# The end of a hybrid attention, state-space and expert block: gate matmuls, weight splits and the final scaling in another order

## The chip, the cores and the metric

The kernel runs on one core of a Trainium2 chip. The metric is the device time of one execution in microseconds. TensorE (PE) does the matmuls, VectorE (DVE), ScalarE (ACT) and GpSimd (POOL) the rest, and SyncE (SP) issues the loads and stores. TensorE's clock has two levels, 2.4 and 1.2 GHz; the profile shows the granted one as 1.00 or 0.50.

## The reference

One token block of 256 x 1024 goes through a norm, an attention branch and a state-space branch, a mixture of 16 experts, and at the end a gated projection of a second input and a last norm. What the change touches is the end:

```python
        h2 = rms_norm(x, ffn_norm_g[i])
        x = x + hier_moe(h2, w_rg[i], b_rg[i], w_re[i], b_re[i], w_gate[i], w_up[i], w_down[i])
        x = x + jax.nn.sigmoid(x @ w_ple_gate[i]) * (p[i] @ w_ple_proj[i])
    return rms_norm(x, final_norm_g)
```

`hier_moe` sums, over experts, a weight per token times `(silu(h @ w_gate[e]) * (h @ w_up[e])) @ w_down[e]`. `x @ w_ple_gate` is 256 x 1024 by 1024 x 1024.

## The kernel before

The 256 tokens are two tiles `i` = 0, 1 of 128 partitions (`xt[0]`, `xt[1]`), and the 1024 columns are worked on in halves (512) or quarters (256). Experts are handled in batches; the last two batches (numbers 4 and 5, members 8 to 11 and 12 to 15) are what is left when the end begins. Their down projections bring rows of tokens that were gathered for an expert, and a matmul with a selection matrix `st` scatters them back onto the tokens:

- `half_down` (L1450) is batch 4's down projection for one half, in PE line L1455; `q_down` (L1463) is batch 5's for one quarter, PE line L1467. Both end in `q_ev` (L1445): ACT writes the scaled result's high part `yh` (L1447), DVE the remainder `yl` (L1448), so that two fast matmuls together keep full precision.
- `scatter` (PE line L1215) and `q_x2` (PE line L1531) add `yh` and `yl` onto the tokens in PSUM. `q_x2` then adds the sum to the tokens on DVE (L1535).
- `q_T` transposes the finished quarter of x on PE (L1541) and splits it into `x2h` (ACT, L1543) and `x2l` (DVE, L1544).

The gate projection has eight blocks c = 0 to 7 of 128 rows of `w_ple_gate`. Block c needs quarter c // 2 of x: blocks 4 and 5 quarter 2, blocks 6 and 7 quarter 3. `pg_split(c)` splits the block's weights into a high part `wh_pg` (ACT, L377) and a low part `wl_pg` (DVE, L380). `pg(c, i, hfs)` issues its matmuls for token tile i and the halves named: three each (L389 with `wh` and `x2h`, L390 with `wl` and `x2h`, L391 with `wh` and `x2l`). So a block is twelve matmuls of 512 columns, and all eight blocks 96. There are four PSUM accumulators, one for each tile and half; the last two blocks are therefore done accumulator by accumulator (`last_two`, L1635), so that the sigmoids can begin when the first is full.

`pg_gate` (L1567) takes the sigmoid on ACT (L1570), and multiplies and adds on DVE (L1571, L1572). `pg_sq` (L1574) sums squares on ACT (L1577), `pg_sum` (L1580) adds them on DVE (L1581), `pg_pow` (L1584) takes the power -1/2 on POOL (L1586). `pg_gain` (L1588) multiplies with the last norm's gain (L1590), `pg_out` (L1592) with gain and reciprocal root at once (L1594), `store` (L1598) issues the store on SP (L1600).

What sets the order: `manual_schedule` leaves every engine the order in which the code is written, and each engine works through its own instructions in that order, waiting on semaphores for the others. Loads are issued on SP from a list, when a slot of on-chip memory is free, eight in flight at most: four d_r (8 loads, for `half_down(..., "r", 1)`), d_2 (4 loads, for `q_down(2)`), pg 4 and 5, the gain `fng`, d_3 (4 loads, for `q_down(3)`), pg 6 and 7, in this order.

The order of the end before the change, at L1603 to L1667: all of blocks 0 to 2 and half of 3, the r half's projection, the other half of block 3, the scatter, then quarter 2 (projection, scatter, transposes), blocks 4 and 5 with quarter 3's projection among them, quarter 3's scatter and transposes, and the last two blocks.

Of the kernel before, what the change touches and what calls it, by code (L numbers as in the profile page):

```python
# [11 lines left out]
AF = mybir.ActivationFunctionType  # L12
# [17 lines left out]
NB = len(WIDTH)  # L30
# [62 lines left out]
def emit(ctx, tc, ring, x, p, mix_norm_g, w_in, conv_w, conv_b, dt_bias,  # L93
# [1114 lines left out]
    def scatter(pr, mo, st, tiles, halves=(0, 1)):  # L1208
        for i in tiles:
            for hf in halves:  # L1210
                for n, y in enumerate(("yh", "yl")):
                    j, first = 2 * i + hf, pr == 0 and n == 0
                    if first:
                        bx[j] = bank(j, f"x2_{j}")
                    pe.matmul(bx[j], st[:, i * P:(i + 1) * P], mo[y][:, 512 * hf:512 * hf + 512],  # L1215
                              start=first, stop=False, skip_group_check=True)
# [233 lines left out]
    def half_down(pr, hT, cw, n, hf):  # L1450

        b = bank(4, f"y{n}{pr}")
        for c in range(4):
            for s, e in enumerate(members(pr)):
                pe.matmul(b[part(pr, s), :], hT[:, c, part(pr, s)], ready[f"d{e}_{n}{c // 2}"][0][:, c % 2, :],  # L1455
                          start=(c == 0), stop=(c == 3), skip_group_check=True)
            if c % 2:
                for e in members(pr):
                    consumed(f"d{e}_{n}{c // 2}")
        for q in range(2):  # L1460
            q_ev(b, cw, 2 * hf + q, 256 * q)
# [86 lines left out]
    def pg_split(c):  # L1548
        pgw[c] = split(f"pg_{c}", 1) + ([],)
        lows.pop()()  # L1550

    def pg(c, i, hfs=(0, 1)):
        _, _, a, b, done = pgw[c]
        for hf in hfs:
            if c == 0:
                pgb[i, hf] = bank(2 * i, f"pg{i}") if hf == 0 else accbank(f"pg{i}1")
            w, s = slice(512 * hf, 512 * hf + 512), slice(i * P, (i + 1) * P)
            three(pgb[i, hf], X2H.k(c)[:, s], X2L.k(c)[:, s], a[:, 0, w], b[:, 0, w], c == 0, c == KD - 1, True)
            done.append(hf)
        if len(done) == 4:  # L1560
            for t in pgw[c][:2]:
                t.free()
# [26 lines left out]
        t = sc.t[i][:, 512 * h:512 * h + 512]  # L1589
        dve.tensor_tensor(t, t, ready["fng"][0][:, 0, 512 * h:512 * h + 512], OP.mult)  # L1590

    def pg_out(h):  # L1592
        t = sc.t[0][:, 512 * h:512 * h + 512]
        dve.scalar_tensor_tensor(t, t, stat[:, 40:41], ready["fng"][0][:, 0, 512 * h:512 * h + 512], op0=OP.mult,  # L1594
                                 op1=OP.mult)
        store(0, h)

    def store(i, h):  # L1598
        s = slice(512 * h, 512 * h + 512)
        sp.dma_start(dram(out, i * P * D + 512 * h, [[D, P], [1, 512]]), sc.t[i][:, s])  # L1600
# [9 lines left out]
    pg_split(2)  # L1610
    pg(0, 1)
    pg_split(3)
    for c in (1, 2):
        for i in range(2):
            pg(c, i)
    pg(3, 0)
    half_down(NB - 2, hT_a, pend[2], "r", 1)
    pg(3, 1)
    scatter(pend[0], mo, pend[1], (0, 1), (1,))
    q_down(2)  # L1620
    pg_split(4)
    q_x2(2)
    q_T(2)
    pg_split(5)
    pg(4, 0)
    pg(5, 0)
    pg(4, 1)
    q_down(3)
    pg(5, 1)
    q_x2(3)  # L1630
    pg_split(6)
    q_T(3)
    pg_split(7)

    def last_two(i, hf):  # L1635
        for c in (6, 7):
# [4 lines left out]
    last_two(0, 1)  # L1641
    pg_gate(0, 1)
    pg_sq(0, 0)
    last_two(1, 0)
    pg_gate(1, 0)
    pg_sq(0, 1)
# [5 lines left out]
    pg_sq(1, 0)  # L1652
    pg_sq(1, 1, 0)
    pg_sq(1, 1, 1)
    pg_out(0)
    pg_gain(1, 0)
    pg_sum(1)
    r = stat[:, 41:42]
    dve.tensor_tensor(r, stat[:, 38:39], r, OP.add)
    pg_pow(1)  # L1660
    pg_gain(1, 1)
    t = [sc.t[1][:, 512 * h:512 * h + 512] for h in range(2)]
    act.activation(t[0], t[0], AF.Copy, scale=r)
    dve.tensor_scalar(t[1], t[1], r, None, op0=OP.mult)
    for h in range(2):
        store(1, h)
    pg_out(1)  # L1667
    consumed("fng")
    for a in X:
        a.free()  # L1670
# [28 lines left out]
```

## Time and profile before

| | us |
|---|---|
| median of 3 runs | 505.53 (501.83 to 506.48) |
| profiled execution, its time | 504.57 |
| its span, first to last instruction | 502.5 |
| PE busy in the span | 466.6 |
| DVE, ACT, POOL busy | 210.8, 183.0, 122.8 |

Times in the rows are microseconds from the start of the span. In a timeline a row is: start, duration, engine, line, operation, output and inputs by the program's names, shapes, count, and in brackets how long the engine had been idle and what it waited for. PEld is a weight load, which runs beside the matmuls; a "q" behind an engine's name is its sequencer. Matmuls overlap, so a matmul's own duration is longer than the step from one to the next.

### The profile page before, as it was taken

Reading aid. Unit: us, or ns where it says so; the run is one execution under the profiler, and the core shown is the slowest. Engines: PE = TensorE matmul, PEld = TensorE weight load, DVE = VectorE, ACT = ScalarE, POOL = GpSimd, SP = SyncE. Lnnn points to the kernel's source line nnn. Section 1 sums busy time; section 2 is a strip of 40 time slices with the busy share of each in tenths; the row PEclk is TensorE's granted clock in tenths of the full one; section 3 lists DMA queues with packets and bytes.
Section 4 is the critical chain, followed back from the end, with each engine's and each line's share of the span. In section 5 each row is a group of like instructions: output and inputs, shape, how many; then the busy total and the mean of one; then the engine's idle time right before and its main releaser. Section 6 shows DMA issues by size and latency. Waiting matters only on the chain.

```text
span 502.5 us, 8090 instructions
## 1 busy us (share of the span) xinstructions
PE 466.6 (93%) x3001; PEld 321.6 (64%) x3001; DVE 210.8 (42%) x413; ACT 183.0 (36%) x333; POOL 122.8 (24%) x82
## 2 busy tenths in 40 slices
PE   6999999999999999999999999999999588889781
PEld 5997998999988999988744353534322111155551
DVE  5423687795669584744644111111100000060345
ACT  5546577634687263443531111111100000140233
POOL 3847535333788640050400000000000000000001
PEclk8899999999999999999999999999999899989787
DMA  9899997522323798677569999999999999999602
GB/s 294 235 348 349 348 349 232 180 71 59 112 87 125 244 400 275 233 243 302 210 208 331 393 410 407 409 409 409 410 404 394 405 410 408 390 392 372 222 0 84
DMA packets 73271, 145.25 MB, mean 289 GB/s; under 512 B 8245, under 2 KB 41353, under 8 KB 73225
## 3 DMA queue, kind: packets, MB, share of 16 engines
q1 hardware_dynamic: 73080, 144.15, 79.9%
q8 instruction: 25, 0.41, 0.3%
q10 hardware_dynamic: 144, 0.52, 0.3%
q14 instruction: 22, 0.17, 0.1%
HBM read 143.61 MB, written 1.05 MB: 288 GB/s over the span
## 4 chain that ended last, share of the span: by engine, by line
PE 66%; DMA 21%; DVE 7%; ACT 2%; issue 2%; POOL 0%; POOLq 0%; DVEq 0%; SPq 0%; ACTq 0%
DMA u<-in_w_up_dram 8%; DMA g<-in_w_gate_dram 6%; PE g L1168 6%; PE ac_gb L411 5%; PE ac_ob L411 5%; PE ac_ga L411 5%; PE u L1168 4%; PE y L1198 4%; DMA d_h<-in_w_down_dram 4%; PE ac_xs L411 3%; PE ac_q L411 3%; PE ac_bc L411 2%; PE ac_z L411 2%; PE ac_k L411 2%; PE g L1111 2%; DMA pg<-in_w_ple_gate_dram 2%
## 5 line engine op out<-in xcount | busy, mean ns | idle before, releaser
L1586 POOL TENSOR_TENSOR stat<-stat,nhalf 128x1 f32<-128x1 f32 x2 | 1.6, 786 | 250.8 <-DVE stat L1581 248.2
L1168 PE MATMUL u<-u,XT 128*64 128x512 f32 (+1 forms) x256 | 55.7, 598 | 3.3 <-DMA u<-in_w_up_dram 3.1
L1168 PE MATMUL g<-g,XT 128*64 128x512 f32 (+1 forms) x256 | 50.0, 620 | 6.5 <-PEq L1245 4.7
L1168 PEld LDWEIGHTS u<-u,XT 128*64 128x64 f32 (+1 forms) x256 | 14.2, 123 | 40.4 <-issue 21.6
L1168 PEld LDWEIGHTS g<-g,XT 128*64 128x64 f32 (+1 forms) x256 | 13.9, 127 | 40.0 <-issue 30.7
L1198 PE MATMUL y<-d,mid 128*64 128x512 f32 x128 | 28.3, 595 | 0.0
L1181 DVE SCALAR_TENSOR_TENSOR mid<-u,cwt,mid 128x512 f32<-128x512 f32 x6 | 4.5, 751 | 50.5 <-issue 49.3
L380 POOL TENSOR_TENSOR wl_xs<-xs,wh_xs 128x1024 fp32r<-128x1024 f32 x8 | 19.1, 2392 | 17.7 <-ACT wh_xs L377 12.6
L1144 ACT ACTIVATE sT<-st 128x256 fp32r<-128x256 f32 x6 | 2.3, 385 | 53.3 <-DVE cwt L1143 51.0
L1205 DVE SCALAR_TENSOR_TENSOR yl<-y,cwt,yh 128x512 fp32r<-128x512 f32 x8 | 6.0, 750 | 34.0 <-ACT yh L1204 33.6
L1140 DVE COPY cwt<-st 128x1 f32<-128x1 f32 x6 | 0.9, 158 | 45.7 <-PE st L1135 45.7
L1198 PEld LDWEIGHTS y<-d,mid 128*64 128x64 f32 x128 | 8.8, 137 | 16.7 <-issue 15.1
L759 POOL TENSOR_TENSOR su<-su,su 128x768 f32<-128x768 f32 x8 | 16.9, 2110 | 7.6 <-ACT su L758 7.1
L389 PE MATMUL pg<-wh_pg,x2h 128*128 128x512 f32 x32 | 15.2, 474 | 1.4 <-ACT x2h L1543 1.4
L1188 ACT ACTIVATE mid<-hT 128x512 f32<-128x512 f32 x5 | 3.0, 598 | 34.5 <-PE hT L1187 34.5
L380 POOL TENSOR_TENSOR wl_wo<-wo,wh_wo 128x1024 fp32r<-128x1024 f32 x3 | 7.8, 2615 | 31.0 <-ACT wh_wo L377 29.6
L390 PE MATMUL pg<-wl_pg,x2h 128*128 128x512 f32 x32 | 14.5, 452 | 0.8 <-DVE wl_pg L380 0.8
L391 PE MATMUL pg<-wh_pg,x2l 128*128 128x512 f32 x32 | 14.1, 442 | 0.0
L1204 ACT ACTIVATE yh<-y,cwt 128x512 fp32r<-128x512 f32 x8 | 5.5, 688 | 22.5 <-PE y L1198 22.5
L380 POOL TENSOR_TENSOR wl_z<-z,wh_z 128x1024 fp32r<-128x1024 f32 x4 | 9.6, 2401 | 16.3 <-ACT wh_z L377 7.1
L1119 ACT ACTIVATE XT<-g,gfd 128x256 f32<-128x256 f32 x12 | 5.0, 471 | 21.0 <-PE g L1111 19.8
L1111 PE MATMUL g<-S,h2h 128*128 128x256 f32 x44 | 11.5, 295 | 0.6 <-ACT XT L1119 0.6
(414 smaller groups left out, 1176.7 us busy)
## 6 DMA issues: line engine op xcount, KB each, us to landing
g<-in_w_gate_dram SPq DMA_DIRECT2D x64, 512.0 KB, 10.1
u<-in_w_up_dram SPq DMA_DIRECT2D x64, 512.0 KB, 10.1
d<-in_w_down_dram SPq DMA_DIRECT2D x40, 512.0 KB, 9.7
d_h<-in_w_down_dram SPq DMA_DIRECT2D x16, 512.0 KB, 10.4
xs<-in_w_in_dram SPq DMA_DIRECT2D x8, 512.0 KB, 9.9
z<-in_w_in_dram SPq DMA_DIRECT2D x8, 512.0 KB, 8.7
ga<-in_w_in_dram SPq DMA_DIRECT2D x8, 512.0 KB, 8.7
gb<-in_w_in_dram SPq DMA_DIRECT2D x8, 512.0 KB, 4.9
```

What stands on the lines that cost most here:

```text
L380: (pool if pool_lo else dve).tensor_tensor(l, src, h.bitcast(F32), OP.subtract)
L389: pe.matmul(o, lh, rh, start=start, stop=False, skip_group_check=skip)
L390: pe.matmul(o, lh, rl, start=False, stop=False, skip_group_check=skip)
L391: pe.matmul(o, ll, rh, start=False, stop=stop, skip_group_check=skip)
L411: pe.matmul(st["b"][:, T * f:T * f + T], w[:, k, 128 * f:128 * f + 128], x_.k(kk), start=(n + kk + f == 0), stop=(n == 2 and kk == 4 * k_u ...
L759: pool.tensor_tensor(e, e, cbm[:, t // 4:t // 4 + 1, :].to_broadcast([P, 2, 384]), OP.mult)
L1111: pe.matmul(b[:, 256 * k:256 * k + 256], MO[hs, i].t[0][:, kk * P:(kk + 1) * P], S, start=(first and n == 0 and k == 0), stop=(last and n ...
L1119: act.activation(o[:, 256 * k:256 * k + 256], b[:, 256 * k:256 * k + 256], AF.Copy, scale=g2[:, k:k + 1])
L1168: pe.matmul(b[part(pr, s), :], xg.k(kk)[:, part(pr, s, s0)], ready[f"{w}{e}_{c}"][0][:, k, :], start=(kk == 0), stop=(kk == KD - 1), skip_ ...
L1198: pe.matmul(by[hf][part(pr, s), :], mo["hT"][:, c, part(pr, s)], w[:, 0, 512 * hf:512 * hf + 512], start=(c == 0), stop=(c == 3), skip_gro ...
L1204: act.activation(mo["yh"][:, sl], by[hf], AF.Copy, scale=cw)
L1205: dve.scalar_tensor_tensor(mo["yl"][:, sl], by[hf], cw, mo["yh"][:, sl].bitcast(F32), op0=OP.mult, op1=OP.subtract)
```

## The change

The matmuls of the gate projection and the splits of its weights are issued in another order around the two last quarters, and the last norm's products are assigned and ordered differently. No instruction of PE, ACT, POOL or SP is added or taken away; DVE loses one.

```diff
-    for c in (1, 2):
-        for i in range(2):
-            pg(c, i)
+    pg(1, 0)
+    pg(1, 1)
+    pg(2, 0)
+    half_down(NB - 2, hT_a, pend[2], "r", 1)
+    pg(2, 1)
+    scatter(pend[0], mo, pend[1], (0, 1), (1,))
     pg(3, 0)
-    half_down(NB - 2, hT_a, pend[2], "r", 1)
-    pg(3, 1)
-    scatter(pend[0], mo, pend[1], (0, 1), (1,))
     q_down(2)
     pg_split(4)
+    pg(3, 1)
     q_x2(2)
     q_T(2)
     pg_split(5)
     pg(4, 0)
     pg(5, 0)
-    pg(4, 1)
+    pg_split(6)
+    pg_split(7)
     q_down(3)
-    pg(5, 1)
+    pg(4, 1, (0,))
     q_x2(3)
-    pg_split(6)
+    pg(4, 1, (1,))
     q_T(3)
-    pg_split(7)
+    pg(5, 1, (0,))
...
     last_two(0, 1)
     pg_gate(0, 1)
     pg_sq(0, 0)
+    pg(5, 1, (1,))
     last_two(1, 0)
...
     pg_sq(1, 1, 1)
-    pg_out(0)
     pg_gain(1, 0)
     pg_sum(1)
     r = stat[:, 41:42]
     dve.tensor_tensor(r, stat[:, 38:39], r, OP.add)
     pg_pow(1)
-    pg_gain(1, 1)
-    t = [sc.t[1][:, 512 * h:512 * h + 512] for h in range(2)]
-    act.activation(t[0], t[0], AF.Copy, scale=r)
-    dve.tensor_scalar(t[1], t[1], r, None, op0=OP.mult)
-    for h in range(2):
-        store(1, h)
-    pg_out(1)
+    pg_out(0, 0)
+    t = sc.t[1][:, 0:512]
+    act.activation(t, t, AF.Copy, scale=r)
+    pg_out(1, 1)
+    store(1, 0)
+    pg_out(0, 1)
```

`pg_out` now takes the token tile as well: `pg_out(i, h)`.

On PE, behind quarter 2's down projection (L1467, output `y`), there stood the scatter (L1531) and the transposes (L1541) directly, then block 4's first matmul:

```order
L1467 MATMUL y_5992<-d_2_5770,hTb_5838 32x256
L1467 MATMUL y_5992<-d_2_5772,hTb_5838 32x256
L1531 MATMUL x_1_3292<-yh_3142,sT_3040 128x256
L1531 MATMUL x_1_3292<-yl_3143,sT_3040 128x256
L1531 MATMUL x_3_3325<-yh_3142,sT_3040 128x256
L1531 MATMUL x_3_3325<-yl_3143,sT_3040 128x256
L1541 MATMUL x2T_6021<-ident,x_66 128x128 x2
L1541 MATMUL x2T_6021<-ident,x_67 128x128 x2
L389 MATMUL pg_5907<-wh_pg_6011,x2h_6026 128x512
```

Now six matmuls of block 3, token tile 1, stand between the projection and the scatter (pg_5919 and pg_5923 are tile 1's two accumulators):

```order
L1467 MATMUL y_5986<-d_2_5772,hTb_5838 32x256
L389 MATMUL pg_5919<-wh_pg_5927,x2h_5892 128x512
L390 MATMUL pg_5919<-wl_pg_5928,x2h_5892 128x512
L391 MATMUL pg_5919<-wh_pg_5927,x2l_5893 128x512
L389 MATMUL pg_5923<-wh_pg_5927,x2h_5892 128x512
L390 MATMUL pg_5923<-wl_pg_5928,x2h_5892 128x512
L391 MATMUL pg_5923<-wh_pg_5927,x2l_5893 128x512
L1531 MATMUL x_1_3292<-yh_3142,sT_3040 128x256
L1531 MATMUL x_1_3292<-yl_3143,sT_3040 128x256
L1531 MATMUL x_3_3325<-yh_3142,sT_3040 128x256
L1531 MATMUL x_3_3325<-yl_3143,sT_3040 128x256
L1541 MATMUL x2T_6021<-ident,x_66 128x128 x2
```

These six stood ahead of the projection before. In the same way nine matmuls of blocks 4 and 5 that stood ahead of quarter 3's scatter now stand around its scatter and transposes, and three of block 5 behind the second accumulator of the last two blocks.

On ACT, around the eviction of quarter 3 (L1447), the two last splits (L377, blocks 6 and 7) stood behind the eviction, the second behind the split of x (L1543) too; now both stand ahead of it:

```order
 L377 ACTIVATE wh_pg_6030<-pg_5797 128x1024
-L1447 ACTIVATE yh_3142<-y_6052,cwt 128x256
-L377 ACTIVATE wh_pg_6083<-pg_5817 128x1024
-L1543 ACTIVATE x2h_6026<-x2T_6087 128x512
-L377 ACTIVATE wh_pg_6094<-pg_5827 128x1024
-L1570 ACTIVATE sc_6104<-pg_5907 128x512
-L1570 ACTIVATE sc_6104<-pg_5911 128x512
-L1577 ACTIVATE pg_5907,stat<-sc_6104 128x512
+L377 ACTIVATE wh_pg_6046<-pg_5817 128x1024
+L377 ACTIVATE wh_pg_6050<-pg_5827 128x1024
+L1447 ACTIVATE yh_3142<-y_6054,cwt 128x256
+L1543 ACTIVATE x2h_6026<-x2T_6085 128x512
```

DVE's low splits (L380) moved in the same way, ahead of the eviction's low part (L1448) and the additions (L1535). The L1570 and L1577 rows are the first gates; they keep their places.

On DVE, at the very end, behind the last gate (L1572), with `stat` the column of sums, sc_6104 (now sc_6101) token tile 0 and sc_6124 token tile 1:

```order
-L1594 SCALAR_TENSOR_TENSOR sc_6104<-sc_6104,stat,fng 128x512
 L1590 TENSOR_TENSOR sc_6124<-sc_6124,fng 128x512
 L1581 TENSOR_SCALAR stat<-stat 128x1
-L1659 TENSOR_TENSOR stat<-stat 128x1
-L1590 TENSOR_TENSOR sc_6124<-sc_6124,fng 128x512
-L1664 TENSOR_SCALAR sc_6124<-sc_6124,stat 128x512
-L1594 SCALAR_TENSOR_TENSOR sc_6104<-sc_6104,stat,fng 128x512
-L1695 UNCONDITIONAL_BRANCH
+L1661 TENSOR_TENSOR stat<-stat 128x1
+L1594 SCALAR_TENSOR_TENSOR sc_6101<-sc_6101,stat,fng 128x512
+L1594 SCALAR_TENSOR_TENSOR sc_6124<-sc_6124,stat,fng 128x512
+L1594 SCALAR_TENSOR_TENSOR sc_6101<-sc_6101,stat,fng 128x512
```

Tile 0's first scaling moved behind the sums, and tile 1's second half is scaled and gained in one instruction. SP's loads stand in the same order as before; of its four stores only those of tile 1's two halves changed places.

## Rows read from the trace of the kernel before

**Rows 1.** The page, chain that ended last: shares of the span by engine.

```profile
PE 66%; DMA 21%; DVE 7%; ACT 2%; issue 2%; POOL 0%; POOLq 0%; DVEq 0%; SPq 0%; ACTq 0%
```

**Rows 2.** Windows: length, busy (count) of PE, PEld, DVE, ACT, POOL; PEclk, DMA share, GB/s.

```profile
445.20:448.50 3.30, 3.09 (x12) 2.36 (x11) 2.49 (x5) 1.79 (x3) 0.00 (x0) 0.50 1.07 390
448.60:457.40 8.80, 8.80 (x39) 7.00 (x38) 3.52 (x4) 2.14 (x3) 0.00 (x0) 1.00 1.07 371
466.05:469.05 3.00, 1.00 (x4) 0.60 (x4) 1.90 (x3) 1.42 (x2) 0.00 (x0) 1.00 1.10 354
469.10:472.40 3.30, 2.47 (x7) 1.78 (x8) 1.54 (x4) 1.54 (x2) 0.00 (x0) 0.50 0.89 331
472.40:475.80 3.40, 3.40 (x9) 2.63 (x8) 0.80 (x1) 0.00 (x0) 0.00 (x0) 0.50 0.12 51
479.50:482.60 3.10, 2.82 (x18) 2.06 (x14) 1.66 (x4) 1.42 (x2) 0.00 (x0) 1.00 0.00 0
482.70:486.10 3.40, 1.99 (x6) 1.16 (x7) 2.53 (x3) 1.55 (x2) 0.00 (x0) 1.00 0.00 0
486.20:489.50 3.30, 3.30 (x9) 2.59 (x8) 1.39 (x2) 1.16 (x3) 0.00 (x0) 0.50 0.00 0
```

**Rows 3.** Timeline of quarter 2, from its down projection to block 4.

```profile
464.12 1.93 PE L1467 MATMUL y<-d,hTb 128*32 128x256 f32 x32
...
466.69 0.48 DVE L1448 SCALAR_TENSOR_TENSOR yl<-y,cwt,yh 128x256 fp32r<-128x256 f32 x1 [3.52 <-ACT yh L1447]
...
467.63 1.23 DVE L380 TENSOR_TENSOR wl_pg<-pg,wh_pg 128x1024 fp32r<-128x1024 f32 x1 [0.46 <-ACT wh_pg L377]
468.77 0.75 DVE L1535 TENSOR_TENSOR x<-x,x 128x256 f32<-128x256 f32 x2
...
469.25 1.11 PE L1541 MATMUL x2T<-ident,x 128*128 128x128 f32 x4 [1.41 <-DVE x L1535]
...
471.05 0.79 PE L389 MATMUL pg<-wh_pg,x2h 128*128 128x512 f32 x1 [0.69 <-ACT x2h L1543]
```

**Rows 4.** Timeline of quarter 3, from its down projection to blocks 6 and 7.

```profile
477.63 1.93 PE L1467 MATMUL y<-d,hTb 128*32 128x256 f32 x32
...
481.43 0.76 DVE L1535 TENSOR_TENSOR x<-x,x 128x256 f32<-128x256 f32 x2 [0.80 <-PE x L1531]
...
481.90 0.77 PE L1541 MATMUL x2T<-ident,x 128*128 128x128 f32 x4 [0.28 <-DVE x L1535]
...
484.09 0.50 PE L391 MATMUL pg<-wh_pg,x2l 128*128 128x512 f32 x1
...
485.57 0.50 PE L390 MATMUL pg<-wl_pg,x2h 128*128 128x512 f32 x1 [0.75 <-DVE wl_pg L380]
```

**Rows 5.** Chain of waits, one gate matmul at each clock: start, share of the chain.

```profile
457.28 0.23 PE pg L391
...
473.12 0.43 PE pg L390
```

**Rows 6.** Loads: issues on SP's timeline; the pg tile's landing and its high split.

```profile
442.57 3.19 SPq L160 DMA_DIRECT2D d_r<-in_w_down_dram  x3
...
447.86 6.03 SPq L160 DMA_DIRECT2D d<-in_w_down_dram  x3
...
466.16 0.35 SPq L160 DMA_DIRECT2D pg<-in_w_ple_gate_dram  x1
...
L377 ACT ACTIVATE wh_pg<-pg x8: 1047/1050/1054, 443.4 to 483.2; 128x1024 fp32r<-128x1024 f32 x8
...
DMA to landing us min/median/max: 8.2/9.3/10.7
```

**Rows 7.** Timeline of the end: last accumulator of squares, and the sum.

```profile
494.88 0.19 ACT L1577 ACTIVATION_READ_ACCUMULATOR pg<-sc 128x1 f32 x1
...
495.64 0.20 DVE L1581 TENSOR_SCALAR stat<-stat 128x1 f32<-128x1 f32 x1
```

**Rows 8.** Window as in rows 2, without POOL, of the transposes (tile x2T) alone.

```profile
445.20:448.50 3.30, 1.86 (x8) 1.01 (x6) 1.26 (x2) 1.20 (x2) 0.50 1.07 390
```

More of the change, by code (lines that the diff above doesn't have):

```diff
@@ L1590, in pg_gain, with pg_out @@
         dve.tensor_tensor(t, t, ready["fng"][0][:, 0, 512 * h:512 * h + 512], OP.mult)
[L1592 to L1596, printed above, removed]
+    def pg_out(i, h):
+        t = sc.t[i][:, 512 * h:512 * h + 512]
+        dve.scalar_tensor_tensor(t, t, stat[:, 40 + i:41 + i], ready["fng"][0][:, 0, 512 * h:512 * h + 512],
+                                 op0=OP.mult, op1=OP.mult)
+        store(i, h)
     def store(i, h):
```

## The prediction

> **What bounds the kernel now.** I read the chain of waits of the whole page first, then stage windows of the last 60 us, then the timeline of the two places where PE stands still. By the chain PE holds 66% of the span and DMA 21% [rows 1]; of the tail that the change touches, the last DMA has landed by about 474.4, and from 448.6 to the end the path is PE and the short relays PE, ACT, DVE, PE. The windows show where PE is idle: between 466.05 and 469.05 it works 1.00 us of 3.00, and between 482.70 and 486.10 1.99 of 3.40 [rows 2]. After each of the two the granted clock is 0.50, that is 1.2 GHz in place of 2.4, from 469.1 to 475.8 and from 486.2 to 489.5 [rows 2]. One 512-column matmul of the gate projection (the pg matmuls) is then issued every 0.43 us, not 0.23 [rows 5]. So an idle stretch is paid twice: as waiting, and as slow matmuls behind it. Those are the terms.
>
> The first relay, quarter 2: its down projection ends at 464.12 + 1.93 = 466.05, the low part of its eviction runs from 466.69 to 467.17, the additions to x start at 468.77 behind the low split of gate block 4 (467.63, 1.23), the transposes at 469.25 take 1.11, and the first matmul of block 4 starts at 471.05 [rows 3]. That is 5.00 us in which PE has nothing but the scatter and the transposes. The second relay, quarter 3: down projection until 477.63 + 1.93 = 479.56, additions at 481.43, transposes until 482.67, then PE waits for the low half of x at 484.09 and for the low split of block 7 at 485.57 [rows 4].
>
> **The change part by part.** No matmul is added or removed. All times below are in the profiled execution's own clock.
>
> (a) Order ahead of quarter 2. The r half's down projection and the scatter now stand twelve gate matmuls earlier, six of them return before the down projection, and six stand behind it. That projection ends 6 x 0.23 = 1.4 us sooner, at 464.7. Two transfers must have landed. The last d_r issue ended at 442.57 + 3.19 = 445.8 and took at least 0.3, so with the longest landing of the pg loads, 10.7, it is there at 456.2 [rows 6]; the projection starts at 457.51 - 12 x 0.23 = 454.8 [rows 5] on the loads issued four earlier and comes to this one half-way, so between 0 and 1.4, and I take 0. The last d_2 issue ended at 453.89 [rows 6]; counted from 453.6, it lands between 461.8 (8.2) and 464.3 (10.7), and PE wants it at 462.8: a cost of 0 to 1.5. Most landings lie at the median of 9.3, which is 462.9; I take 0.
>
> (b) Relay of quarter 2 with six gate matmuls behind the down projection. ACT and DVE have the same instructions in the same order, and the additions wait for the low split of block 4, not for PE: 468.77 - 466.05 = 2.72 after the projection's end [rows 3]. PE needs 1.4 for the six and about 0.5 for the scatter's four of 256 columns, under 2.0 in all, inside these 2.72. So the relay still takes 5.00, and block 4 starts at 469.7. One thing more: the transposes now stand at 467.9 to 468.7, before the time at which the clock fell (469.05), and at full clock four of them take 0.77 instead of 1.11 [rows 3, 4]. That gives 0.3: 469.35, or 1.7 sooner than 471.05.
>
> (c) From there to the end of quarter 3's down projection. Before: 471.05 to 479.56, with 18 gate matmuls. Now: 12, the other six are kept back. What they cost hangs on when the clock comes back. Two low stretches in which PE worked nearly throughout (3.09 of 3.30, 3.30 of 3.30) ended at 448.6 and 489.5; the one from 469.1, of whose first 3.30 PE worked 2.47, lasted twice as long, to 475.8 [rows 2]. Now PE would work some 3.05 of these 3.30, which is near the 3.09. Early return (about 472.5): 7 x 0.43 + 5 x 0.23 + 1.93 ends at 475.5. Late return (475.9): 12 x 0.43 ends at 474.5, the projection's first 1.4 us run at half rate, and it ends at 477.1. So 4.1 or 2.5 sooner.
>
> (d) Relay of quarter 3. The two last splits now stand on ACT and DVE ahead of the eviction, which adds a wait: ACT stands at block 7's split until its load has landed, 466.16 + 8.2 = 474.4 (the shortest landing belongs to the last issue, which has nothing behind it), and needs 1.05 [rows 6], so 475.45. DVE's low split then takes 1.23, until 476.7. Queued behind are the eviction, its low part, the additions and every later gate. The low part of the eviction began 0.64 and ended 1.12 after the projection's end before [rows 3]. In the early case it is held from 476.15 to 476.7 and ends at 477.2; in the late case nothing is held and it ends at 477.1 + 1.1 = 478.2. Then some 0.7 for the rest of the scatter (an estimate from rows 5: three halves of 0.23, and a matmul's 0.4 until its result is there), additions at 477.9 (478.9), and from the additions to PE's matmul on the low half of x the 484.09 - 481.43 = 2.66 of before [rows 4]: 480.55 (481.55). Beside it PE has three matmuls behind the projection, three before the transposes and three behind: 9 x 0.23 = 2.05 of cover. The wait at 485.57 is gone, since both splits were over by 476.7. Four more matmuls end the first of the last four blocks at 481.45 (482.45); before, two behind 485.57 ended it at about 486.05. So 4.6 (3.6) sooner.
>
> (e) The rest of PE. Before, 18 matmuls from there, eight of them low (486.2 to 489.5) [rows 2]: 8 x 0.43 + 10 x 0.23 = 5.7. Now 21, the three kept back among them, at 0.23: 4.8, if the clock holds. That is 0.9 more: 5.5 (4.5) sooner. If the clock falls once more in quarter 3's relay, eight matmuls cost 0.2 each more: 1.6.
>
> (f) Last scaling. The sum of squares stood at 495.64 behind the scaling of token tile 0, while the last accumulator was read at 494.88 + 0.19 = 495.07 [rows 7]. With that scaling moved behind the sum, the reciprocal root and the last three stores come 0.57 sooner. The first tile's first store leaves later, beside nothing else: between 0 and 0.5 lost if it meets the other three; I take 0. What lies between PE's end and the sum, the last gates on ACT and DVE, is as before; the three matmuls kept back give the gates ahead of them 0.7 more room.
>
> Sum: -5.5 - 0.6 = -6.1 (early), -5.1 (late), -4.5 (early, and a second fall). The clock's change is not tied to a place in the kernel, so the executions will mix these: I take the middle of the outer two, (-6.1 - 4.5) / 2 = -5.3, beside which the late case lies. The profiled execution took 504.57, of which 502.5 is span: 504.57 - 5.3 = 499.3, which is 1.05% less. The three runs shown have the median 505.53, 1.0 above it, and spread from 501.83 to 506.48, so -2.7 to +1.9 around it. About 1% is what a measurement of this kernel can tell from no change.
>
> **A rule weighed against the trace.** In the stretch 445.20 to 448.50 PE was busy 3.09 us, of which 1.86 were transposes [rows 8], and at 448.6 the clock was back at full. The Trainium skill (page "TensorE: Matmul & The Clock Gate", Part 4: PE-mode transpose) says that the full rate does not engage for transposes, because they do not count as busy in the same way. By the trace they did count here; by the rule the relays, whose PE time is partly transposes, would stay poor whatever is filled in, the second fall would be the rule and not the exception, and the sum would be that of the first rival.
>
> **The rivals.**
> First: the clock is low in both relays and late in coming back. For it: the nine fillers still leave PE some 0.9 us idle before the low part of the eviction (0.3 in the late case) and 0.3 before the low half of x, and 1.99 of 3.40 was too little [rows 2]. Against: 2.82 of 3.10 was enough [rows 2], and that relay had only six fillers. Price: -5.1 + 1.6 = -3.5, so 501.1.
> Second: term (a) does not come about, because d_2 lands as late as 464.3. Then PE stands 1.4 at the projection; -5.3 + 1.4 = -3.9, so 500.7. For it: the load is wanted 1.4 sooner than before and nothing loads it sooner, the order on SP is the same. Against: the median landing.
> Third, the slower side: the splits put in front of the eviction hold it until block 7 has landed. From a landing at 474.4 on, each us of lateness is a us of the end, as ACT and DVE are in order and the low part of the eviction ends 2.8 after it. The gain is gone at 474.4 + 5.3 = 479.7; at 482 the time is 504.57 + 2.3 = 506.9. For it: before, the same block was not wanted until 483. Against: the longest landing of a pg load, 10.7, makes it 476.9 [rows 6], which costs 2.5 and leaves -2.8.
>
> **How the numbers follow.** Forecast 0.78 (498.5 to 500.1 by itself), first rival 0.12, second 0.06, third 0.04. Of the forecast's -6.1 to -4.5 two thirds lie beyond 1%, which is 5.05 us: 0.52 faster. The rest of it and the first two rivals: 0.44 the same. The third, 0.04, slower. The range goes from 504.57 - 6.1 - 2.1 (most of the spread below) = 496.4 to 501.1 + 1.9 = 503.0.
>
> **What would show it.** Right: the first matmul of block 4 starts 1.7 sooner; no PE wait on the low split of block 7; splits of blocks 6 and 7 on ACT end near 475.5 and the eviction follows; the last pg matmul starts about 5.5 sooner; the sum of squares follows the last accumulator at once. Wrong: a clock of 0.50 from 469 to the end of quarter 3 and again behind it (first rival); PE idle before the d_2 projection (second); ACT idle before block 7's split for over 3 us with PE waiting behind it (third).

## The result and the profile after

The changed kernel took 498.39 us (median of 4 runs, 496.42 to 499.90) against 504.84 us for the kernel before (median of 4, the three runs shown above among them). The ratio is 0.9891, with a 95% interval from 0.9846 to 0.9937. Two later comparisons, each with its own runs of the kernel before, gave 0.9928 [0.9902, 0.9955] and 0.9896 [0.9856, 0.9936]. So the change saves 3.6 to 6.5 us by the medians; 5.3 was forecast. The profiled execution of the changed kernel took 496.42, the fastest of its four; its span is 494.4.

Two executions never reach the end at the same moment of the span, because they differ already in the parts that the change doesn't touch. So I anchor both at the last down projection ahead of the changed order: the half projection of batch 5 (L1455, `yh<-d_h`), which ended at 439.95 + 1.90 = 441.85 before and at 437.83 + 1.90 = 439.73 after. The other anchor is the last gate matmul. First the timeline of before at the two anchors, then of after:

```profile
439.95 1.90 PE L1455 MATMUL yh<-d_h,hTb 128*32 128x512 f32 x10 [0.30 <-DMA d_h<-in_w_down_dram]
...
491.65 0.40 PE L391 MATMUL pg<-wh_pg,x2l 128*128 128x512 f32 x1
```

```profile
437.83 1.90 PE L1455 MATMUL yh<-d_h,hTb 128*32 128x512 f32 x10 [0.31 <-DMA d_h<-in_w_down_dram]
...
452.42 3.64 PE L1455 MATMUL yr<-d_r,mid 128*32 128x512 f32 x32
...
460.47 1.93 PE L1467 MATMUL y<-d,hTb 128*32 128x256 f32 x32
...
465.13 0.75 DVE L1535 TENSOR_TENSOR x<-x,x 128x256 f32<-128x256 f32 x2
465.60 0.77 PE L1541 MATMUL x2T<-ident,x 128*128 128x128 f32 x4 [1.15 <-DVE x L1535]
...
467.06 0.50 PE L389 MATMUL pg<-wh_pg,x2h 128*128 128x512 f32 x1 [0.69 <-ACT x2h L1543]
...
470.62 1.93 PE L1467 MATMUL y<-d,hTb 128*32 128x256 f32 x32
...
472.42 2.46 DVE L380 TENSOR_TENSOR wl_pg<-pg,wh_pg 128x1024 fp32r<-128x1024 f32 x2 [3.20 <-ACT wh_pg L377]
...
472.56 1.06 ACT L377 ACTIVATE wh_pg<-pg 128x1024 fp32r<-128x1024 f32 x1 [0.18 <-DMA pg<-in_w_ple_gate_dram]
...
473.53 0.46 ACT L1447 ACTIVATE yh<-y,cwt 128x256 fp32r<-128x256 f32 x1
474.03 0.38 PE L1531 MATMUL x<-yh,sT 128*128 128x256 f32 x1 [0.58 <-ACT yh L1447]
474.80 0.48 DVE L1448 SCALAR_TENSOR_TENSOR yl<-y,cwt,yh 128x256 fp32r<-128x256 f32 x1
475.33 0.39 PE L1531 MATMUL x<-yl,sT 128*128 128x256 f32 x1 [0.91 <-DVE yl L1448]
...
479.51 0.39 PE L389 MATMUL pg<-wh_pg,x2h 128*128 128x512 f32 x1
...
484.05 0.39 PE L391 MATMUL pg<-wh_pg,x2l 128*128 128x512 f32 x1
```

What to see here, beside [rows 3] and [rows 4]: neither projection (452.42, 460.47) has a bracket, so PE waited for no load. The transposes of quarter 2 take 0.77 us instead of 1.11, since the clock is full. The 0.75 us wait for the low split of block 7 (485.57 before) is gone. A new wait stands in its place, in two pieces: 0.58 us at 474.03, where PE needs the high part `yh`, which ACT began only at 473.53, behind block 7's split, and 0.91 us at 475.33, where PE needs the low part `yl`, which DVE began only at 474.80, behind the two low splits. Block 7's split itself (472.56) waited for the block's load.

From anchor to last gate matmul it took 492.05 - 441.85 = 50.2 us before and 484.44 - 439.73 = 44.7 after. From there to the end of the span, 502.5 - 492.05 = 10.45 and 494.4 - 484.44 = 9.96. Together the tail is 6.0 us shorter, by these two executions.

Two windows of after, columns as in [rows 2]: the stretch behind the anchor, and quarter 2's relay:

```profile
442.80:446.10 3.30, 3.30 (x14) 2.65 (x13) 2.48 (x5) 1.51 (x3) 0.00 (x0) 0.50 1.05 387
462.40:467.05 4.65, 2.83 (x15) 2.00 (x14) 2.38 (x5) 2.07 (x4) 0.00 (x0) 1.00 1.09 353
```

In this execution the clock is low only once, at the beginning, ahead of what the change touches. In the relay of quarter 2 (the second row) PE now works 2.83 of 4.65 us where it had worked 1.00 of the first 3.00, and no low stretch follows; in `again`, below, one does follow.

At the end (answers [rows 7]) the sum of squares follows the last accumulator at once, 487.39 behind 487.29; before it stood 0.76 us behind it:

```profile
487.29 0.19 ACT L1577 ACTIVATION_READ_ACCUMULATOR pg<-sc 128x1 f32 x1
487.39 0.21 DVE L1581 TENSOR_SCALAR stat<-stat 128x1 f32<-128x1 f32 x1
```

### The profile page after: what moved, and what is told of

It reads as the page before. It is cut to its first block, busy times and chain, and to the rows that moved or that the text cites. A ratio compares the mean times of both kernels' runs of the same rounds, so it can differ in the third digit from the quotient of the medians.

```text
span 494.4 us, 8088 instructions
## 1 busy us (share of the span) xinstructions
PE 462.0 (93%) x3001; PEld 318.7 (64%) x3001; DVE 208.5 (42%) x412; ACT 183.2 (37%) x333; POOL 122.9 (25%) x82
## 4 chain that ended last, share of the span: by engine, by line
PE 72%; DMA 17%; DVE 6%; ACT 2%; issue 1%; POOL 0%; POOLq 0%; DVEq 0%; SPq 0%; ACTq 0%
PE g L1168 7%; DMA u<-in_w_up_dram 6%; PE y L1198 6%; PE u L1168 6%; PE ac_gb L411 5%; PE ac_ob L411 5%; PE ac_ga L411 5%; DMA d_h<-in_w_down_dram 4%; DMA g<-in_w_gate_dram 4%; PE ac_xs L411 3%; PE ac_q L411 2%; PE ac_bc L411 2%; PE ac_z L411 2%; PE g L1111 2%; PE ac_k L411 2%; DMA pg<-in_w_ple_gate_dram 2%
## 5 line engine op out<-in xcount | busy, mean ns | idle before, releaser
L1168 PEld LDWEIGHTS g<-g,XT 128*64 128x64 f32 (+1 forms) x256 | 14.6, 130 | 38.8 <-issue 31.0
L380 POOL TENSOR_TENSOR wl_xs<-xs,wh_xs 128x1024 fp32r<-128x1024 f32 x8 | 19.2, 2396 | 17.7 <-ACT wh_xs L377 7.8
L380 POOL TENSOR_TENSOR wl_wo<-wo,wh_wo 128x1024 fp32r<-128x1024 f32 x3 | 7.8, 2615 | 31.0 <-ACT wh_wo L377 29.6
L389 PE MATMUL pg<-wh_pg,x2h 128*128 128x512 f32 x32 | 13.5, 423 | 0.7 <-ACT x2h L1543 0.7
L380 POOL TENSOR_TENSOR wl_z<-z,wh_z 128x1024 fp32r<-128x1024 f32 x4 | 9.6, 2405 | 16.3 <-ACT wh_z L377 7.1
L390 PE MATMUL pg<-wl_pg,x2h 128*128 128x512 f32 x32 | 12.9, 402 | 0.1
L391 PE MATMUL pg<-wh_pg,x2l 128*128 128x512 f32 x32 | 12.8, 401 | 0.0
## 6 DMA issues: line engine op xcount, KB each, us to landing
d_h<-in_w_down_dram SPq DMA_DIRECT2D x16, 512.0 KB, 10.4
```

The costliest lines, as they stand in the source:

```text
L380: (pool if pool_lo else dve).tensor_tensor(l, src, h.bitcast(F32), OP.subtract)
L389: pe.matmul(o, lh, rh, start=start, stop=False, skip_group_check=skip)
L390: pe.matmul(o, lh, rl, start=False, stop=False, skip_group_check=skip)
L391: pe.matmul(o, ll, rh, start=False, stop=stop, skip_group_check=skip)
L1168: pe.matmul(b[part(pr, s), :], xg.k(kk)[:, part(pr, s, s0)], ready[f"{w}{e}_{c}"][0][:, k, :], start=(kk == 0), stop=(kk == KD - 1), skip_ ...
```

## The experiments

The theory: the time comes from three places, the second quarter's order (terms a and b, with the clock of c), the third quarter's (d, e) and the last scaling (f). The main rival: most of it is the clock alone, which stays high because PE has something to do in the relays, whatever that is. A further one: moving the splits ahead of the eviction costs what the fillers bring.

### Both kernels once more

Four runs are of unaltered kernels: the changed one (`again`, `after_c`) and the one before (`before_b`, `before_c`, one execution each).

> The changed kernel once more, unaltered. If the low clock was avoided for good by the fillers, the trace shows 1.00 through both relays again and the time stays near 496 to 498. If it depends on where the clock's changes happen to fall, as I hold, some executions show a stretch at 0.50 in a relay and lie 2 to 3 us higher; the runs then spread over 496 to 500 and the ratio to the kernel before stays at 0.987 to 0.991.

> The kernel before once more, unaltered, for its trace. If the two low stretches of the profiled execution (469.1 to 475.8, 486.1 to 489.5) belong to the kernel, they are there again and the end from the last d_h projection is again 60.6 us long. If, as I hold, they depend on where the clock's changes fall, one may be shorter or missing, and the end is 1 to 3 us shorter.

> The kernel before a third time, for its trace. The end from the last d_h projection was 60.6 and 58.9 us long, with 13.7 and 6.8 us at the low clock up to the last gate matmul. I expect a length between 58 and 61 that goes with the time at the low clock, about half a microsecond for each.

> The changed kernel unaltered, beside both_c on the same chip. The two earlier sets of runs gave a ratio to the kernel before of 0.989 and 0.993; I expect 0.990 to 0.993, and a trace whose end from the last d_h projection is 54.6 to 56 us long.

Measured: `again` 498.78 us (10 runs, before 502.36 in 22), 0.9928 [0.9902, 0.9955]; `after_c` 498.32 (6 runs, before 503.76 in 17), 0.9896 [0.9856, 0.9936]; `before_b` 501.58 and `before_c` 500.25. From the anchor to the end of the span it took 58.9 us in `before_b`, as expected, 57.2 in `before_c`, less than the 58 to 61 expected, and 54.0 in `after_c`, less than the 54.6 to 56. `again` spread from 496.2 to 501.0 us, and its ratio lies just above the 0.987 to 0.991 expected; its trace has a stretch at 0.50, but from the anchor to the end of the span that execution took 54.8 us, only 0.2 more than after, where 2 to 3 were expected.

The windows say more, PEclk being the third number from the right. They start at the 25th gate matmul, up to which both orders have done the same work, and end with the last gate matmul; so a low stretch ahead of the change is left out. The first fence is the kernel before in its first profile, then each in a fence of its own `before_b`, `before_c`, after, `again`, `after_c`:

```profile
453.27:492.05 38.78, 34.12 (x189) 21.43 (x187) 13.01 (x19) 9.90 (x17) 0.00 (x0) 0.87 0.53 182
```

```profile
451.21:489.06 37.85, 33.20 (x189) 20.62 (x187) 13.01 (x19) 9.91 (x17) 0.00 (x0) 0.91 0.55 190
```

```profile
451.63:487.70 36.07, 31.41 (x189) 19.57 (x187) 12.89 (x19) 9.83 (x16) 0.00 (x0) 0.95 0.57 198
```

```profile
450.97:484.44 33.47, 30.03 (x189) 18.17 (x187) 12.95 (x19) 10.13 (x17) 0.00 (x0) 1.00 0.63 218
```

```profile
452.80:485.87 33.07, 30.81 (x189) 19.16 (x187) 12.96 (x19) 10.24 (x17) 0.00 (x0) 0.95 0.60 208
```

```profile
454.29:487.04 32.75, 29.90 (x189) 18.07 (x187) 12.97 (x19) 10.12 (x17) 0.00 (x0) 1.00 0.62 215
```

The same kernel needed 38.8, 37.9 and 36.1 us for the same work. A mean clock of 0.87 means that 2 x 0.13 of the stretch, some 10 us, ran at 1.2 GHz; 0.91 means 6.8 us and 0.95 some 3.6. Each further 3.3 us or so of low clock made the stretch 0.9 to 1.8 us longer. So the execution on which the prediction stood was the poorest of the three in this part. The fair comparison is at one clock: `before_c` and `again` each fall once, behind the same relay, and take 36.1 and 33.1 us. By this pair the order itself saves 3.0 us ahead of the last gate matmul, and the last scaling its 0.5 behind it. The rest, up to 2.7 us, hangs on how often the clock falls in the execution of before that is taken.

The clock of `before_b` and `before_c` differs behind the relay of quarter 3. First `before_b`, then `before_c`:

```profile
469.25:472.55 3.30, 3.30 (x9) 2.50 (x9) 1.29 (x2) 0.29 (x1) 0.00 (x0) 0.50 0.43 173
482.90:486.20 3.30, 3.30 (x9) 2.55 (x9) 1.38 (x2) 0.60 (x1) 0.00 (x0) 0.50 0.00 0
```

```profile
469.05:472.35 3.30, 3.28 (x8) 2.59 (x9) 1.91 (x2) 0.91 (x1) 0.00 (x0) 0.50 0.54 216
480.50:487.60 7.10, 6.19 (x24) 4.35 (x24) 5.29 (x8) 3.91 (x8) 0.00 (x0) 1.00 0.00 0
```

Both fall behind quarter 2's relay and come back after 3.3 us; only one falls a second time. The order of the instructions is the same, so it alone doesn't decide whether the clock falls.

`again` shows the other case of the changed kernel, in which the clock does fall behind quarter 2's relay, although PE worked 2.84 of 4.65 us in it, as in after:

```profile
464.20:468.85 4.65, 2.84 (x17) 2.01 (x14) 2.38 (x4) 2.05 (x4) 0.00 (x0) 1.00 1.10 358
469.15:472.45 3.30, 3.30 (x9) 2.31 (x9) 1.62 (x2) 0.61 (x1) 0.00 (x0) 0.50 0.64 250
...
475.40:482.40 7.00, 6.63 (x30) 4.73 (x31) 3.37 (x6) 1.67 (x3) 0.00 (x0) 1.00 0.00 0
```

PE arrives later at quarter 3's eviction, and waits only 0.36 us for its low part:

```profile
473.44 1.93 PE L1467 MATMUL y<-d,hTb 128*32 128x256 f32 x32
...
473.99 1.06 ACT L377 ACTIVATE wh_pg<-pg 128x1024 fp32r<-128x1024 f32 x1 [0.18 <-DMA pg<-in_w_ple_gate_dram]
...
476.23 0.48 DVE L1448 SCALAR_TENSOR_TENSOR yl<-y,cwt,yh 128x256 fp32r<-128x256 f32 x1
476.76 0.39 PE L1531 MATMUL x<-yl,sT 128*128 128x256 f32 x1 [0.36 <-DVE yl L1448]
...
480.95 0.39 PE L389 MATMUL pg<-wh_pg,x2h 128*128 128x512 f32 x1
```

The same rows of `after_c`:

```profile
473.94 1.93 PE L1467 MATMUL y<-d,hTb 128*32 128x256 f32 x32
...
475.12 1.06 ACT L377 ACTIVATE wh_pg<-pg 128x1024 fp32r<-128x1024 f32 x1 [0.18 <-DMA pg<-in_w_ple_gate_dram]
...
477.35 0.48 DVE L1448 SCALAR_TENSOR_TENSOR yl<-y,cwt,yh 128x256 fp32r<-128x256 f32 x1
```

Set side by side, the three executions of the changed kernel have one thing in common. Block 7's split starts when its load has landed (472.56, 473.99, 475.12). The low part `yl` starts 2.24, 2.24 and 2.23 us later, and the last gate matmul ends 11.88, 11.88 and 11.92 us after that landing, whether the clock fell before or not. So in the changed kernel this load sets the end, and not the clock: `again`, at 1.2 GHz for some 3.3 us, takes 33.1 us from the 25th gate matmul on, between the 33.5 and 32.8 of the two whose clock stayed full.

### One part alone

Quarter 2 alone (`quarter2_only`), edited from the kernel before:

```diff
-    for c in (1, 2):
-        for i in range(2):
-            pg(c, i)
-    pg(3, 0)
+    pg(1, 0)
+    pg(1, 1)
+    pg(2, 0)
     half_down(NB - 2, hT_a, pend[2], "r", 1)
-    pg(3, 1)
+    pg(2, 1)
     scatter(pend[0], mo, pend[1], (0, 1), (1,))
+    pg(3, 0)
     q_down(2)
     pg_split(4)
+    pg(3, 1)
     q_x2(2)
```

> The kernel before with the reordering around quarter 2 alone (r half and scatter earlier, half of block 3 behind the projection); quarter 3, the splits and the last scaling as before. My theory: block 4 starts 1.7 us sooner, and the low stretch behind the relay is shorter or missing, which gives 0 to 2 us more: 1.5 to 3.5 less in all, with PE still waiting 1.2 us for the low half of x and block 7's low split. Rival (the fill around quarter 3 carries it): under 1 us less.

Measured: 500.62 us (12 runs), 0.9939 [0.9902, 0.9975], so some 3.1 us of the medians, inside the 1.5 to 3.5 expected. In its trace the clock stays full through quarter 2's relay and falls behind quarter 3's, where nothing was filled in:

```profile
466.00:473.00 7.00, 5.12 (x23) 3.27 (x22) 3.81 (x5) 1.69 (x3) 0.00 (x0) 1.00 0.99 342
482.10:485.40 3.30, 3.30 (x8) 2.62 (x9) 1.38 (x2) 0.60 (x1) 0.00 (x0) 0.50 0.00 0
```

The splits alone (`splits_only`), edited from the kernel before; the old places of both splits are removed:

```diff
     pg(4, 1)
+    pg_split(6)
+    pg_split(7)
     q_down(3)
```

> The kernel before with one part of the change: the splits of blocks 6 and 7 queued ahead of quarter 3's projection and eviction; matmul order and last scaling as before. My theory: the projection ends late enough here (479.6 in the kernel before, against 475.5 for the split) that nothing is held back; the waits on the low half of x and on block 7's low split shrink from 1.2 to about 0.4, so 0.8 less, and 1.6 more if the clock then holds behind quarter 3's relay: 0.8 to 2.4 us less. Rival (the splits carry the change): 4 us less.

Measured: 500.26 us (12 runs, before 502.21 in 23), 0.9964 [0.9935, 0.9993]: about 1.9 us, as the theory has it, with an interval that just leaves out no change. In its trace the wait for block 7's low split is gone, and the clock holds from 475.4 to the last gate matmul, although it was low before that:

```profile
468.60:475.30 6.70, 5.67 (x15) 4.22 (x16) 3.45 (x5) 3.36 (x4) 0.00 (x0) 0.50 0.64 234
475.40:488.90 13.50, 12.54 (x78) 8.54 (x77) 6.67 (x11) 4.15 (x9) 0.00 (x0) 1.00 0.00 1
```

The last scaling alone (`scaling_only`), the kernel before with the new `pg_out` and the new last lines:

```diff
-    pg_gain(1, 1)
-    t = [sc.t[1][:, 512 * h:512 * h + 512] for h in range(2)]
-    act.activation(t[0], t[0], AF.Copy, scale=r)
-    dve.tensor_scalar(t[1], t[1], r, None, op0=OP.mult)
-    for h in range(2):
-        store(1, h)
-    pg_out(1)
+    pg_out(0, 0)
+    t = sc.t[1][:, 0:512]
+    act.activation(t, t, AF.Copy, scale=r)
+    pg_out(1, 1)
+    store(1, 0)
+    pg_out(0, 1)
```

> The kernel before with the last scaling of the changed one alone. My theory: the stretch from the last gate matmul's end to the span's end shrinks from 10.45 to 9.9 us, by 0.5 to 0.6; the whole time by as much, less than its spread. Rival (the first store, now later, meets the other three): no change.

Measured: 501.00 us (10 runs), 0.9977 [0.9941, 1.0012]. In time it can't be told from no change; in the trace it can. From the last gate matmul to the end of the span it takes 9.9 us, against 10.4 to 10.5 in the three traces of before, and the sum follows the accumulator by 0.10 us:

```profile
494.21 0.19 ACT L1577 ACTIVATION_READ_ACCUMULATOR pg<-sc 128x1 f32 x1
494.31 0.21 DVE L1581 TENSOR_SCALAR stat<-stat 128x1 f32<-128x1 f32 x1
```

The fillers without the splits and the scaling (`fill_only`): PE's order of the changed kernel, but the splits at their old places and the old end:

```diff
-    pg_split(6)
-    pg_split(7)
     q_down(3)
     pg(4, 1, (0,))
     q_x2(3)
+    pg_split(6)
     pg(4, 1, (1,))
     q_T(3)
+    pg_split(7)
```

> The kernel before with the matmul order of the changed one, but with the splits of blocks 6 and 7 where they stood (behind the eviction and behind the transposes) and the old last scaling. My theory: most of the gain is the matmuls held back, so 3.4 to 5 us less than before, with PE waiting on the low split of block 7 again. Rival (the splits queued ahead carry the gain): 1.5 us less at most.

Measured: 499.65 us (5 runs), 0.9934 [0.9902, 0.9966], so 2.7 us by the medians and 3.3 by the ratio, just under the 3.4 to 5 expected. PE again waits for the last low split, as before the change:

```profile
482.93 0.50 PE L390 MATMUL pg<-wl_pg,x2h 128*128 128x512 f32 x1 [0.75 <-DVE wl_pg L380]
```

So by the medians the fillers bring most of it (2.7 of the 3.6 us of `again`, on the same chip), the splits take away one wait, and the scaling half a microsecond. The medians of the single parts (3.1 + 1.9 + 1.2 = 6.2) can't be added up to the whole: the fillers around quarter 3 were never run alone, and the intervals are each some 3 us wide or more.

### The clock alone

`spare` is the kernel before with 13 matmuls on operands at hand, in the same relays, whose result nobody reads; nothing is left out:

```diff
+    def spare(c, n):
+        b = bank(5, f"spare{c}{n}")
+        for j in range(n):
+            pe.matmul(b, X2H.k(0)[:, 0:P], pgw[c][2][:, 0, 0:512], start=True, stop=True, skip_group_check=True)
...
     q_x2(2)
+    spare(4, 6)
     q_T(2)
+    spare(4, 2)
...
     q_x2(3)
+    spare(5, 2)
     q_T(3)
+    spare(5, 3)
```

> The kernel before in its own order, with thirteen spare matmuls of 512 columns, whose result nobody reads, put into the gaps of the two relays (six before and two behind quarter 2's transposes, two before and three behind quarter 3's). Nothing useful is moved. If the clock is a part of its own, as I hold, it stays at 1.00 in the relays and the time falls by 2 to 4 us although PE has 13 matmuls more. Rival (only the useful work moved into the gaps counts): no change, or up to 1 us longer.

Measured: 501.63 us (10 runs, before 502.36), 0.9972 [0.9947, 0.9998], so 0.7 us by the medians and 1.4 by the ratio, less than the 2 to 4 that the theory expected. Its windows: the stretch in which the clock was low ahead of the relays, and from the 25th gate matmul to the last:

```profile
447.10:450.40 3.30, 2.87 (x10) 2.20 (x9) 2.32 (x5) 2.04 (x4) 0.00 (x0) 0.50 1.06 387
454.99:490.11 35.12, 33.25 (x202) 20.30 (x200) 12.92 (x19) 9.83 (x17) 0.00 (x0) 1.00 0.58 201
```

With useless work in the relays the clock is 1.00 through both of them to the last gate matmul, and the stretch takes 35.1 us, where the three executions of before took 36.1 to 38.8 and the changed kernel 32.8 to 33.5. So the clock was held by filling alone, in the one trace taken, and the stretch was 1.0 to 3.7 us shorter with it; but the changed kernel is another 1.6 to 2.4 us shorter. That remainder fits the fillers of the change being work that then no longer stands elsewhere, and the splits. By time, 0.7 us is less than half of the 3.6 of `again`, but the intervals of 0.9972 and 0.9928 still touch. So the rival that it is the clock and nothing else falls; which of the two parts is the larger is not settled.

### Without the new wait

In the changed kernel block 7's split holds the eviction. Put behind the scatter (`split7_behind`):

```diff
     pg_split(6)
-    pg_split(7)
     q_down(3)
     pg(4, 1, (0,))
     q_x2(3)
+    pg_split(7)
```

> The changed kernel with block 7's split moved behind the eviction of quarter 3 and its scatter; block 6's split stays ahead. My theory: ACT and DVE no longer hold the eviction until block 7's load has landed, its low part ends about 1.2 us sooner after the projection, and the tail from quarter 3's projection to the end is 0.9 to 1.3 us shorter than in the changed kernel, with block 7's low split still done before PE wants it. Rival: the low split of block 7 becomes the last wait again, as in the kernel before, and the tail is the same or up to 0.5 longer.

Measured: 498.18 us (6 runs), 0.9906 [0.9874, 0.9939], beside 0.9928 for the changed kernel on the same chip. In the trace the hold is gone: `yl` starts 0.58 us behind the projection's end at 477.04, and DVE's last low split, at 479.26, is done before PE asks for it. But in this execution the clock had fallen behind quarter 2's relay, as in `again`, so the projection ended late, the case in which the changed kernel has little to wait for: there `yl` started 0.86 us behind it. From the projection's end to the end of the span it took 20.3 us, beside 20.4 in `again`, so the 0.9 to 1.3 us that were expected are not shown:

```profile
475.11 1.93 PE L1467 MATMUL y<-d,hTb 128*32 128x256 f32 x32
...
477.62 0.48 DVE L1448 SCALAR_TENSOR_TENSOR yl<-y,cwt,yh 128x256 fp32r<-128x256 f32 x1 [1.09 <-ACT yh L1447]
...
479.26 1.22 DVE L380 TENSOR_TENSOR wl_pg<-pg,wh_pg 128x1024 fp32r<-128x1024 f32 x1
```

The same thing for quarter 2, in addition (`both_behind`, and once more as `both_c` beside `after_c`): there the additions to x wait for block 4's low split, by term (b), so that split goes behind the scatter too.

```diff
     q_down(2)
-    pg_split(4)
     pg(3, 1)
     q_x2(2)
+    pg_split(4)
     q_T(2)
```

> The changed kernel with block 7's split behind the eviction, as in split7_behind, and block 4's split moved behind quarter 2's scatter as well, so that the additions to x no longer wait for its low part. My theory: quarter 2's relay, from the projection's end to block 4's first matmul, shrinks from 4.66 to about 3.9 us, of which 0.2 to 0.3 comes back as a wait on the low half of x: 0.5 less than split7_behind, about 1.2 less than the changed kernel. Rival: quarter 3 then waits for block 6's load and split, and nothing is left of it.

> both_behind unaltered, beside the changed kernel on the same chip. My theory: 0.9 to 1.5 us less than after_c in the median, so a ratio of 0.988 to 0.991. Rival: its 1.0 less so far was the spread of executions, and the two are equal within 0.5 us.

Measured: `both_behind` 497.42 us (6 runs, before 502.21), 0.9901 [0.9864, 0.9937]; `both_c` 496.39 us (6 runs, before 503.76), 0.9854 [0.9812, 0.9896], while `after_c` on the same chip took 498.32. The timeline of `both_c` in quarter 2 and at quarter 3's eviction, and its window from the 25th gate matmul to the last:

```profile
464.67 1.93 PE L1467 MATMUL y<-d,hTb 128*32 128x256 f32 x32
...
468.45 0.76 DVE L1535 TENSOR_TENSOR x<-x,x 128x256 f32<-128x256 f32 x2 [0.73 <-PE x L1531]
...
470.39 0.50 PE L389 MATMUL pg<-wh_pg,x2h 128*128 128x512 f32 x1 [0.69 <-ACT x2h L1543]
...
474.74 1.06 ACT L377 ACTIVATE wh_pg<-pg 128x1024 fp32r<-128x1024 f32 x1 [3.45 <-DMA pg<-in_w_ple_gate_dram]
...
477.50 0.39 PE L1531 MATMUL x<-yl,sT 128*128 128x256 f32 x1 [0.57 <-DVE yl L1448]
```

```profile
455.17:486.64 31.47, 29.81 (x189) 18.15 (x187) 12.87 (x19) 10.12 (x17) 0.00 (x0) 1.00 0.62 216
```

The additions now follow the scatter and not the split, and block 4 starts 470.39 - 466.60 = 3.79 us behind the projection instead of 4.66. The stretch takes 31.5 us, 1.3 to 2.0 less than `after_c` and after, at the same clock of 1.00. The rival comes half true: quarter 3's eviction now waits for block 6. Its load landed at 474.74, `yl` started 2.23 us later, the same step as behind block 7's, and PE waited 0.57 us for it (0.91 in `both_behind`); but the gain was not lost by it. Block 6's split behind the eviction as well was not tried. That this version is faster than the changed kernel by time is likely (1.9 us by the two medians of one chip, more than the 0.9 to 1.5 expected) but not settled: the intervals of 0.9854 and 0.9896 overlap.

All profiled executions side by side, sorted by PE's order: where the clock was low, and the time from the 25th gate matmul to the last. "Short" is a low stretch of about 3.4 us, "long" one of about 6.8.

| run | low ahead of the change | low behind quarter 2's relay | low behind quarter 3's relay | 25th to last, us |
|---|---|---|---|---|
| before | short | long | short | 38.8 |
| `before_b` | no | short | short | 37.9 |
| `before_c` | no | short | no | 36.1 |
| `scaling_only` | no | long | short | 38.6 |
| `splits_only` | no | long | no | 36.0 |
| `spare` | short | no | no | 35.1 |
| `quarter2_only` | short | no | short | 35.3 |
| `fill_only` | short | short | no | 33.8 |
| after | short | no | no | 33.5 |
| `again` | short | short | no | 33.1 |
| `after_c` | short | no | no | 32.8 |
| `split7_behind` | short | short | no | 32.7 |
| `both_behind` | short | no | no | 32.0 |
| `both_c` | short | no | no | 31.5 |

`spare` aside, behind quarter 2's relay the clock fell in all five executions with PE's old order there, and in three of the eight with the new one, each time short. Behind quarter 3's relay it fell in four of the six with the old order there, and in none of the seven with the new one. So the fillers make a fall rarer and shorter; they don't rule it out. The low stretch ahead of the change stands in all eight of the new order and in `spare`, but in one of five of the old: from the anchor to the 25th gate matmul it took 11.2 to 11.8 us with it and 10.6 without. What brings it is not shown; it takes back a part of the gain.

## Why the prediction was right, step by step

**(a) Order ahead of quarter 2: right.** From the start of the r half's projection to the end of quarter 2's it took 462.40 - 452.42 = 9.98 us; before, 466.05 - 457.44 = 8.61. The projection of r came twelve matmuls sooner (2.76 us) and the way behind it is 1.37 longer, which leaves the 1.4. PE waited for no load at either projection, in the three traces of the changed kernel, so the second rival did not occur.

**(b) Relay of quarter 2: right.** 467.06 - 462.40 = 4.66 us, where the working had 469.35 - 464.7 = 4.65. The additions at 465.13 stand 2.73 behind the projection's end (2.72 was taken): it is the split of block 4 that sets them, which `both_c` then confirmed by taking it away.

**(c) The clock: right in part.** `again` is the early case: low for 3.3 us, and from block 4's start at 468.87 to the projection's end at 475.37 it is 6.5 us, where the working had 6.15 (early) and 7.75 (late). In the two other traces of the changed kernel the clock did not fall behind the relay at all, and it took 5.5 us; the working took the fall as given and changed only its length, so it did not have that as a case. On the other side it treated the kernel before as one fixed time: the profiled execution of before had some 10 us at 1.2 GHz from the 25th gate matmul to the last, and two more had 6.8 and 3.6. Measured against that one profile the whole tail is 6.0 us (after) and 5.8 us (`again`) shorter, near the 6.1 of the early case; against `before_c` it is only 2.5 and 2.3. The medians, 3.6 to 6.5, lie between, as they would if the executions of before mix these. That the forecast of -5.3 came so close is therefore in part luck: it was a middle of cases of the changed kernel, set against the poorest execution of before.

**(d) The new wait: the mechanism right, the size from 0.2 to 1.6 us.** The chain of load, split, low split and eviction ran as described. The hold was put at 0.55 us (early) or nothing (late). From the projection's end to the start of `yl` it took 0.64 us before [rows 3], and now 2.25 (after), 1.48 (`after_c`) and 0.86 (`again`): a hold of 1.6, 0.8 and 0.2. To set after beside the working, the 2.12 us between the anchors are added: block 7 had landed at 472.56 + 2.12 = 474.68, 0.3 later than the 474.4 taken, and the projection ended at 474.67, 0.8 sooner than in the early case, since the clock had not fallen. That is the 1.1 between 0.55 and 1.6. From the projection's end to the second of the last blocks, 479.51, it took 6.96 instead of 5.95; in `again`, where PE came late, 480.95 - 475.37 = 5.58. So this wait takes back what a better clock gives: from block 4's start to the projection's end the low clock cost `again` 1.0 us, and from the 25th gate matmul to the last it still took 33.1, between 33.5 and 32.8. That is the third rival's mechanism, at its place and its price per microsecond, since the end followed the landing by 11.9 us in all three; but the load was never late enough to decide the sign. The working had 481.45 + 4.8 - 474.4 = 11.85 us for that distance. This chain, and not the clock, is what the prediction had right to a tenth.

**(e) The rest of PE: right.** From 479.51 to 484.44 is 4.93 us; 4.8 was taken, and the clock held.

**(f) Last scaling: right.** 10.45 to 9.96 between PE's end and the end of the span, 0.49 of the 0.57.

**The first rival** (the clock low in both relays) was not seen in `again`, after or `after_c`; quarter 3's relay stayed at 1.00 in all three. The rule of the Trainium skill that was weighed (page "TensorE: Matmul & The Clock Gate", Part 4: PE-mode transpose) would have had the relays stay poor. Behind the filled relays of after and `after_c` they didn't, and four transposes took 0.77 us at a clock of 1.00 where they took 1.11 at 0.50 [rows 3]; but the relays held gate matmuls beside the transposes, so no run separates what each does to the clock.

## What to carry to other kernels

Fill a relay with work that has to be done anyway, and not only to hold the clock: useless fillers brought 0.3% here, gate matmuls moved into the relays 0.7% (with intervals that overlap). When an instruction that waits for a load is put ahead of one that PE waits for, ask which comes first in the good case, not only in the profiled one; here PE waited 0.36 us where it was late and 0.91, or 0.58 and 0.91, where it was early, and the load, not PE, set the end. And a stretch that runs at two clocks should be read from more than one trace before its low time is booked as gain.

## What was not expected of the hardware

The low time of one and the same kernel from its 25th gate matmul to its last was some 10, 6.8 and 3.6 us in three executions, with 38.8, 37.9 and 36.1 us for the same 189 matmuls. In `before_b` and `before_c` the same order of instructions fell back to 1.2 GHz behind quarter 3's relay once and once not; what decides it is left open.

The stretch ahead of the anchor differs as well: it ended between 439.7 and 443.9 in the traces, although no version changes anything there. That is 4 us, as much as the change itself brings, and the reason why single executions are compared here from anchor to anchor.
